# A two-layer trunk: where the second layer's S5 tables and first modulation vectors are made

## The chip, the cores and the metric

One core of a Trainium2 chip runs the whole kernel. The engines are TensorE (PE, with its weight loads as PEld), VectorE (DVE), ScalarE (ACT), GpSimd (POOL) and SyncE (SP), which here does nothing but issue transfers. The metric is the device time of one execution in microseconds (us), the median over the runs shown.

## The reference, cut to what matters

The input x is 512 tokens of 1024 channels, f32, and one conditioning vector c. Two layers follow one another, each of this form (names as in the reference, cut):

```
mod = silu(c) @ ada_w + ada_b                 # 6 vectors of 1024: shift, scale, gate, twice
h   = rms_norm(x, n1g) * (1 + scale1) + shift1
q, f, i, og, u, ga, gb = h @ w_in             # 56 blocks of 128 columns
a = hgrn2(q, f, i, og)                        # 8 heads, a gated linear recurrence in chunks of 32
s = gelu(s5(u)); s = s * sigmoid(s @ glu_w + glu_b)   # complex diagonal state space
x = x + gate1 * ((sigmoid(ga) * a + sigmoid(gb) * s) @ w_out)
h = rms_norm(x, n2g) * (1 + scale2) + shift2
x = x + gate2 * peer(h)                       # 16384 single-neuron experts, top 16 per head
```

The S5 branch of a layer depends on the layer's parameters alone (a, dt, B, C) for the small matrices with which it is applied: powers of the discretised diagonal, B times them, C times them. The kernel makes these matrices on the chip and calls them tables, 8 per layer, one for each unit of 128 channels. The modulation vectors depend on c and the layer's weights alone. Neither needs x.

## The kernel before, in words

**Precision and order.** Every f32 weight tile of 128x1024 is loaded by SP (tile `raw`), rounded by ACT into `whi` (L114), and DVE forms the rest, `wlo = raw - whi` (L116). Activations are split in the same way into `ahi` (L121, L229) and `alo` (L123, L231). Each product is three matmuls: hi by hi, lo by hi, hi by lo (L132 to L134, L145 to L147 in halves of the tokens, L1041 to L1043 for the V stage). A scheduler that works with a timeline of its own sets the order of instructions on every engine; the buffers of the tile pools decide when a tile may be written again, and a pool that opens in memory that another pool gave back waits for the last user of it. SP issues nearly all loads strictly in its order.

**One layer.** First the norm (L199 to L231), then the mixer: for each of 8 heads the projections, the HGRN2 head, an S5 unit with its table, ending in `yap` (L704); then the gates `ga` and `gb` (L732, L757), the gelu of S5, the glu products (L771 to L777) and the output products w_out with `merge` into x (L781 to L787). Of the eight w_out products five are whole and the last three are done in halves of 256 tokens, so that the second norm (`norm_mod_halves`, L235) can begin on the first half. Then PEER: wq and scores, top-16 selection, a dense matrix of gate values, the U stage (128 dense products with the U table, L795) and the V stage: a loop over 128 slices i, which loads a V tile, splits it, loads and gates the activations A (L1028 to L1032), and runs 24 matmuls of 128x384 into eight accumulators. The last 128 tokens are not done densely: POOL gathers rows of U and V by index (L957), and DVE multiplies and adds them (L967, L978). When all slices are done `into_x` (L1046) adds the accumulators to x.

**The tables.** `s5_small` (L277 to L397) makes, out of a and dt, some 190 small tiles of 128x32. `s5_maps` (L400 to L418) loads bre, bim, cre and cim and forms `bb` and `cc` of 128x512. `s5_build(sm, u, pv, pool, V, G)` (L432 to L482) fills one packed tile of 128x4352 for unit u: products of powers with bb and cc on DVE (L440 to L456), copies by ACT (L443, L464), and small products of 128 by 4 to 128x32 (L475 to L482) on the engine that is given as its last argument. `s5_tables` (L515 to L536) then transposes parts of the tile on PE and makes the matrices of the unit.

**Where this is done for layer 0 and for layer 1.** Layer 0's mixer calls `s5_maps` and `pack_tile` itself, and before each head builds the next head's table with DVE and POOL (`V, G`). Layer 1's tables are made ahead, during layer 0's V stage, by the generator `next_layer(1)` (L801 to L817): one step of it at each fourth slice. Its first step runs `s5_small`, opens the pool `bp`, runs `s5_maps` and `cond`, which makes csil = silu(c); a step then builds one table with DVE alone (`V, V`) and stores it to DRAM (`s5t`); after every second table four chunks of the modulation are made (`ada`, L161: load 128x1024, multiply by csil with a sum on DVE, L165), 16 chunks in all, which are the shift and the scale of the first norm. Layer 1's mixer loads one packed table per head (`pkl`, L713).

**The other chunks.** The 32 remaining chunks of a layer are made in its own mixer by `later(n)`: one in each ga step, three in each glu step, into the tag "ada" (two buffers) of the pool `gp`.

```
for i in range(n_end):                        # L1060, V stage
    w, g = spilled(i)
    for d in range(J):
        vmm(acc[d], d, w, g, i == 0, i == n1 - 1)
    gsteps(2 if i % 8 == 7 else 1)
    if i % 4 == 1:
        next(jobs, None)                      # a step of next_layer(1)
```

Of the kernel before, what the change touches and what calls it, by code (L numbers as in the profile page):

```python
# [4 lines left out]
F32 = mybir.dt.float32  # L5
# [12 lines left out]
J = 8  # L18
NB = 4
L = 2  # L20
# [21 lines left out]
def trunk(tc, a, dbg=None, layers=L, n_i2=128):  # L42
    nc = tc.nc
    V, S, G, TE = nc.vector, nc.scalar, nc.gpsimd, nc.tensor
    uid = [0]

    def nm(s):
        uid[0] += 1
        return f"{s}{uid[0]}"
# [350 lines left out]
    def s5_maps(l, sm, keep, pool, tags):  # L400
        E = V
        br, bi, tmp = (pool.tile([128, 32, 16], F32, tag=t, name=nm(t), bufs=1) for t in tags)
        nc.sync.dma_start(br, a["bre"][l])
        nc.sync.dma_start(bi, a["bim"][l])
        bb = [keep.tile([128, 32, 16], F32, name=nm("bb")) for _ in range(2)]
        zrb, zib = (z[:, :, None].to_broadcast([128, 32, 16]) for z in sm["z"])
        E.tensor_tensor(bb[0], zrb, br, op=OP.mult)
        E.tensor_tensor(tmp, zib, bi, op=OP.mult)
        E.tensor_tensor(bb[0], bb[0], tmp, op=OP.subtract)
        E.tensor_tensor(bb[1], zrb, bi, op=OP.mult)  # L410
        E.tensor_tensor(tmp, zib, br, op=OP.mult)
        E.tensor_tensor(bb[1], bb[1], tmp, op=OP.add)
        cc_ = [keep.tile([128, 32, 16], F32, name=nm("cc")) for _ in range(2)]
        nc.sync.dma_start(cc_[0], a["cre"][l])
        nc.sync.dma_start(cc_[1], a["cim"][l])
        S.activation(cc_[1], cc_[1], AF.Copy, scale=-1.0)
        sm.update(bb=bb, cc=cc_)

    su = drp.tile([L, J, 128, T], F32, name="su")
    sy = drp.tile([L, J, 128, T], F32, name="sy")  # L420
    s5t_ = {l: drp.tile([J, 128, 4352], F32, name=f"s5t{l}") for l in range(1, L)}

    PK = 4352

    def pack_tile(pool):
        t = pool.tile([128, PK], F32, name=nm("pk"))
        G.memset(t, 0.0)
        return t

    def pack_views(t):  # L430
        v = lambda o, m: t[:, o:o + 128 * m].rearrange("p (g m c) -> p g m c", g=4, c=32)
        w = lambda o: t[:, o:o + 512].rearrange("p (g n) -> p g n", g=4)  # L432
        return dict(wes=(v(0, 4), v(512, 4)), cas=(v(1024, 5), v(1664, 5)), bbr=(v(2304, 4), v(2816, 4)),
                    co=w(3328), si=w(3840))
# [49 lines left out]
    def mixer(l, h):  # L484
# [10 lines left out]
        sm = s5s[l]  # L495

        toe = fx.tile([128, 4, 4, 32], F32, name=nm("toe"))
        G.memset(toe, 0.0)
        if l == 0:
            s5_maps(l, sm, fx, hp, ("w1", "w2", "w3"))  # L500
            pk0 = pack_tile(fx)
        dcol = fx.tile([128, 32], F32, name=nm("dcol"))
        for j in range(4):
            nc.sync.dma_start(dcol[32 * j:32 * j + 32, :], a["dsk"][l])
# [200 lines left out]


        def tables(u):
            if l == 0:
                pv = pack_views(pk0)
                s5_build(sm, u, pv, hp, V, G)  # L710
            else:
                t = hp.tile([128, PK], F32, tag="pkl", name=nm("pkl"), bufs=1)
                nc.sync.dma_start(t, s5t_[l][u])  # L713
                pv = pack_views(t)
            return s5_tables(u, pv)

        tb_ = tables(0)
# [11 lines left out]
        def gates(n, pool, **kw):  # L729
            for _ in range(n):  # L730
                t = pool.tile([128, T], F32, name=nm("sgb"), **kw)
                S.activation(t, proj(48 + len(sgb)), AF.Sigmoid)  # L732
                sgb.append(t)

        if l == 0:
            gates(2, smp, tag="h", bufs=2)
        else:
            gates(J, yp)
        hctx.close()
        fx = mctx.enter_context(tc.tile_pool(name=f"gx{l}", bufs=1))  # L740
        hp = mctx.enter_context(tc.tile_pool(name=f"gp{l}", bufs=2))

        if l == 0:
            gates(J - 2, fx)
        else:
            cond(fx, stp)
        todo = list(range(16, 48))

        def later(n):
            n = min(n, len(todo))  # L750
            if n:
                ada(l, [todo.pop(0) for _ in range(n)], hp, "ada")

        for e in range(J):
            ps = proj(40 + e)
# [25 lines left out]
        def merge(e, ps, c=slice(0, T)):  # L781
            V.scalar_tensor_tensor(xT[:, e, c], ps[:, c], mod[l][:, 16 + e:17 + e], xT[:, e, c],
                                   op0=OP.mult, op1=OP.add)

        for e in range(J - 3):
            merge(e, dense(a["wout"][l, e], mg))
        dense_halves([a["wout"][l, e] for e in range(J - 3, J)], mg, lambda n, ps, c: merge(J - 3 + n, ps, c))  # L787
        mctx.close()
# [12 lines left out]
    def next_layer(l, fctx):  # L801
        with tc.tile_pool(name=f"s5s{l}", bufs=1) as t5:
            s5s[l] = s5_small(l, t5, lay[l])
        bp = fctx.enter_context(tc.tile_pool(name=f"bp{l}", bufs=1))
        s5_maps(l, s5s[l], bp, bp, ("cp1", "cp2", "md1"))
        pk = pack_tile(bp)
        cond(bp, stp)
        yield
        for u in range(J):
            s5_build(s5s[l], u, pack_views(pk), bp, V, V)  # L810
            nc.sync.dma_start(s5t_[l][u], pk)
            yield
            if u % 2:
                ada(l, list(range(2 * u - 2, 2 * u + 2)))
                yield
        gain1[l] = col(mod_gain(l, 1, vec["n1g"][:, l, :]))
        shift1[l] = col(mod[l])  # L817

# [401 lines left out]
```

## Time and profile before

| what | us |
|---|---|
| median of 3 runs (lowest to highest) | 3990.93 (3989.17 to 3995.62) |
| the profiled execution | 3988.25 |
| span in the trace | 3986.4 |
| layer 0: heads, yap of the first to yap of the last | 159 to 473 |
| layer 0: w_out, from the first merge to the first half of wq | 592 to 632 |
| layer 0: V stage, first gated slice to the first addition into x | 1421 to 2048 |
| layer 1: norm and first projections, up to yap of the first head | 2075 to 2164 |
| layer 1: heads | 2164 to 2476 |
| layer 1: V stage | 3429 to 3958 |

The profiled execution is 1.85 us longer than its span, and 2.68 us below the median. PE is busy for 94% of the span. In the two layers the same program runs with the same shapes, so a stage of layer 0 can be laid beside the same stage of layer 1; where the two differ in the work that is put beside the matmuls, the trace has both cases. The busy times below are those of an engine's instructions without counting overlaps twice, and the number in brackets is the count of instructions.

### The profile page before, as it was taken

How to read it: one execution, taken by the hardware profiler on the slowest of the kernel's cores; microseconds unless marked ns; L12 is line 12 of the kernel's file. 1: busy time of each engine (PE TensorE's matmuls, PEld its weight loads, DVE VectorE, ACT ScalarE, POOL GpSimd, SP SyncE). 2: the span in 40 equal slices, each digit the busy share in tenths (PEclk: the TensorE clock that was granted, in tenths of full speed). 3: DMA queues.
4: the chain of work that ended last, by engine and by line, in shares of the span. 5: the costliest groups of instructions: out<-in, count | busy, mean ns of one | idle time of the engine just before them, and what ended most of it. 6: DMA issues, size and time to landing. Idle time of an engine off the chain costs nothing.

```text
span 3986.4 us, 62595 instructions
## 1 busy us (share of the span) xinstructions
PE 3737.9 (94%) x21878; PEld 3500.6 (88%) x21878; DVE 3270.8 (82%) x9052; ACT 1577.6 (40%) x2510; POOL 883.7 (22%) x1139
## 2 busy tenths in 40 slices
PE   6999999999999766889999999999999998699998
PEld 5888878999999766888998888789999997699998
DVE  6998787999898889988757777869998988778874
ACT  3454543334343323334434444533334433233332
POOL 7454100022222433341000000000232223332210
PEclk9999999999999778999999999999999998799999
DMA  5222372488898899998743343723799998999984
GB/s 198 71 65 79 117 230 91 131 296 304 321 320 314 289 327 343 364 345 292 273 146 110 120 141 124 253 87 119 270 316 319 319 321 305 324 345 345 348 296 132
DMA packets 371212, 947.55 MB, mean 238 GB/s; under 512 B 36096, under 2 KB 187712, under 8 KB 368848
## 3 DMA queue, kind: packets, MB, share of 16 engines
q1 hardware_dynamic: 250144, 572.74, 42.5%
q0 software_dynamic: 73952, 268.56, 19.6%
q10 hardware_dynamic: 46800, 102.26, 6.7%
q8 instruction: 172, 2.82, 0.3%
q14 instruction: 144, 1.18, 0.1%
HBM read 814.44 MB, written 128.97 MB: 237 GB/s over the span
## 4 chain that ended last, share of the span: by engine, by line
PE 65%; DVE 16%; DMA 11%; issue 4%; ACT 2%; POOL 2%; ACTq 0%; SPq 0%; DVEq 0%; POOLq 0%
PE mm L133 11%; PE mm L132 11%; PE mm L134 11%; DVE wlo L116 3%; DMA gr<-v,idi 3%; PE mm L1042 2%; PE mm L1043 2%; PE mm L1041 2%; DMA gr<-ur,idi 2%; DVE jk L876 2%; DMA ada<-ada 2%; PE pa L1043 2%; PE pa L1042 2%; PE pb L1042 2%; PE pb L1043 2%
## 5 line engine op out<-in xcount | busy, mean ns | idle before, releaser
L114 ACT ACTIVATE whi<-raw 128x1024 fp32r<-128x1024 f32 x688 | 728.6, 1060 | 1354.1 <-PE mm L133 772.8
L133 PE MATMUL mm<-alo,whi 128*128 128x384 f32 (+1 forms) x3360 | 1213.7, 362 | 13.6 <-DVE alo L123 13.4
L134 PE MATMUL mm<-ahi,wlo 128*128 128x384 f32 (+1 forms) x3360 | 1214.1, 362 | 9.4 <-DVE wlo L116 9.1
L132 PE MATMUL mm<-ahi,whi 128*128 128x384 f32 (+1 forms) x3360 | 1213.0, 363 | 6.4 <-ACT ahi L229 5.6
L116 DVE TENSOR_TENSOR wlo<-raw,whi 128x1024 fp32r<-128x1024 f32 x688 | 840.2, 1222 | 254.5 <-ACT whi L114 239.1
L133 PEld LDWEIGHTS mm<-alo,whi 128*128 128x128 f32 x3360 | 636.0, 189 | 64.2 <-DVE alo L123 14.7
L134 PEld LDWEIGHTS mm<-ahi,wlo 128*128 128x128 f32 x3360 | 636.2, 189 | 61.1 <-DVE wlo L116 12.4
L132 PEld LDWEIGHTS mm<-ahi,whi 128*128 128x128 f32 x3360 | 636.6, 190 | 56.8 <-ACT ahi L229 7.1
L957 POOL DMA_INDIRECT gr<-ur,idi x256 | 278.1, 1086 | 1438.1 <-DVE jk L876 384.0
L957 POOL DMA_INDIRECT gr<-v,idi x256 | 362.2, 1415 | 662.7 <-DVE gacc L978 526.0
L978 DVE SCALAR_TENSOR_TENSOR gacc<-gr,gate,gacc 128x1024 f32<-128x1024 f32 x254 | 324.5, 1278 | 51.1 <-DMA gr<-v,idi 50.3
L1041 PE MATMUL mm<-gh,whi 128*128 128x384 f32 x768 | 227.3, 343 | 112.1 <-ACT whi L114 48.4
L967 DVE SCALAR_TENSOR_TENSOR gr<-gr,rows 128x1024 f32<-128x1024 f32 x256 | 311.0, 1217 | 17.6 <-DMA gr<-ur,idi 17.1
L1042 PE MATMUL mm<-gl,whi 128*128 128x384 f32 x768 | 260.9, 342 | 11.1 <-DVE gl L1032 11.0
L1043 PE MATMUL mm<-gh,wlo 128*128 128x384 f32 x768 | 255.9, 339 | 0.2 <-DVE wlo L116 0.2
L1041 PEld LDWEIGHTS mm<-gh,whi 128*128 128x128 f32 x768 | 142.5, 191 | 116.1 <-ACT gh L1030 66.0
L933 PE MATMUL pa<-Q,P 128*128 128x128 f16 x768 | 197.7, 296 | 43.7 <-DVE Q L927 41.1
L1030 ACT ACTIVATE gh<-A 128x384 fp32r<-128x384 f32 x256 | 132.1, 519 | 268.7 <-DVE A L1028 216.8
L876 DVE SCALAR_TENSOR_TENSOR jk<-iof,tf,ci 128x50 f32<-128x50 f32 x1024 | 223.9, 263 | 0.0
L935 ACT ACTIVATE stg<-pa 128x512 f32<-128x512 f32 x192 | 114.4, 598 | 223.3 <-PE pa L934 191.0
L934 PE MATMUL pa<-Q,P 128*128 128x128 f16 x768 | 187.9, 295 | 1.0
L1028 DVE TENSOR_TENSOR A<-A,W 128x384 f32<-128x384 f32 x256 | 139.2, 552 | 57.1 <-DMA A<-sA 52.0
(410 smaller groups left out, 6573.9 us busy)
## 6 DMA issues: line engine op xcount, KB each, us to landing
raw<-u SPq DMA_DIRECT2D x256, 512.0 KB
raw<-v SPq DMA_DIRECT2D x256, 512.0 KB
raw<-win SPq DMA_DIRECT2D x112, 512.0 KB
ada<-ada SPq DMA_DIRECT2D x96, 512.0 KB
sA<-uo ACTq DMA_DIRECT2D x256, 192.0 KB
sW<-stg ACTq DMA_DIRECT2D x64, 768.0 KB
A<-sA SPq DMA_DIRECT2D x256, 192.0 KB
W<-sW SPq DMA_DIRECT2D x64, 768.0 KB
```

Of the source, the lines that this page charges most:

```text
L114: S.activation(hi, raw, AF.Copy)
L116: V.tensor_tensor(lo, raw, hi[:].bitcast(F32), op=OP.subtract)
L132: TE.matmul(ps, hi[:, w], ah, start=(j == 0), stop=False)
L133: TE.matmul(ps, hi[:, w], al, start=False, stop=False)
L134: TE.matmul(ps, lo[:, w], ah, start=False, stop=(j == J - 1))
L876: V.scalar_tensor_tensor(jk, iof[:, 0:NCAND], tf[:, hh, k:k + 1], ci[:, hh], op0=OP.is_equal, op1=OP.mult, accum_out=code[:, hh, k:k + 1])
L957: G.indirect_dma_start(out=g[:], out_offset=None, in_=tab, in_offset=bass.IndirectOffsetOnAxis(ap=ids[:, s_:s_ + 1], axis=0))
L967: V.scalar_tensor_tensor(g, g, 1.0, rows, op0=OP.mult, op1=OP.mult, accum_out=dot[:, s_:s_ + 1])
L978: V.scalar_tensor_tensor(acc_, g, gate[:, s_:s_ + 1], acc_, op0=OP.mult, op1=OP.add)
L1041: TE.matmul(ps, w[0][:, c], g[0], start=first, stop=False)
L1042: TE.matmul(ps, w[0][:, c], g[1], start=False, stop=False)
L1043: TE.matmul(ps, w[1][:, c], g[0], start=False, stop=last)
```

## The change

The tables of layer 1 are no longer made in layer 0's V stage. Layer 1's mixer now does what layer 0's does: `s5_maps` and `pack_tile` at its start, and `s5_build` with `V, G` for each head. The DRAM tiles `s5t`, their stores and their loads are gone. `next_layer(1)` keeps `s5_small` and the two lines at its end. Six of the eight gb gates of layer 1 move from before to after the close of the heads' pools, as in layer 0. The 16 chunks of layer 1's first norm are made in layer 0's w_out loop: four before each of the first four whole products, in the two "ada" buffers, with layer 0's csil.

```
-        if l == 0:
-            s5_maps(l, sm, fx, hp, ("w1", "w2", "w3"))
-            pk0 = pack_tile(fx)
+        s5_maps(l, sm, fx, hp, ("w1", "w2", "w3"))
+        pk0 = pack_tile(fx)
...
         def tables(u):
-            if l == 0:
-                pv = pack_views(pk0)
-                s5_build(sm, u, pv, hp, V, G)
-            else:
-                t = hp.tile([128, PK], F32, tag="pkl", name=nm("pkl"), bufs=1)
-                nc.sync.dma_start(t, s5t_[l][u])
-                pv = pack_views(t)
+            pv = pack_views(pk0)
+            s5_build(sm, u, pv, hp, V, G)
             return s5_tables(u, pv)
...
-        def later(n):
+        follow = list(range(16)) if l + 1 < layers else []
+
+        def later(n, l_=l, todo=todo):
             n = min(n, len(todo))
             if n:
-                ada(l, [todo.pop(0) for _ in range(n)], hp, "ada")
+                ada(l_, [todo.pop(0) for _ in range(n)], hp, "ada")
...
         for e in range(J - 3):
+            later(4, l + 1, follow)
             merge(e, dense(a["wout"][l, e], mg))
...
     def next_layer(l, fctx):
         with tc.tile_pool(name=f"s5s{l}", bufs=1) as t5:
             s5s[l] = s5_small(l, t5, lay[l])
-        bp = fctx.enter_context(tc.tile_pool(name=f"bp{l}", bufs=1))
-        s5_maps(l, s5s[l], bp, bp, ("cp1", "cp2", "md1"))
-        pk = pack_tile(bp)
-        cond(bp, stp)
         yield
-        for u in range(J):
-            s5_build(s5s[l], u, pack_views(pk), bp, V, V)
-            nc.sync.dma_start(s5t_[l][u], pk)
-            yield
-            if u % 2:
-                ada(l, list(range(2 * u - 2, 2 * u + 2)))
-                yield
         gain1[l] = col(mod_gain(l, 1, vec["n1g"][:, l, :]))
```

**DVE in layer 0's V stage.** The names: gacc is the gathered sum of the last 128 tokens (L978 before, L957 after), A, gh and gl the gated activations (L1028 and L1032 before, L1007 and L1011 after), cp and md the table's products. Before:

```order
L165 SCALAR_TENSOR_TENSOR ada3870_17426,mod1_136<-ada3870_17426,csil3542_16003 128x1024
L1028 TENSOR_TENSOR A3889_17519<-A3889_17519,W3890_17521 128x384
L978 SCALAR_TENSOR_TENSOR gacc0_6543<-gr4296_19388,gate1864_8444,gacc0_6543 128x1024
L482 TENSOR_TENSOR pk3540_15999<-md3590_16227,md3591_16228 128x4x4
L456 TENSOR_TENSOR cp3641_16446<-pwr3494_15880,bb3536_15986 128x256
L165 SCALAR_TENSOR_TENSOR ada3871_17429,mod1_136<-ada3871_17429,csil3542_16003 128x1024
L1032 TENSOR_TENSOR gl3884_17484<-A3882_17479,gh3883_17482 128x384
L116 TENSOR_TENSOR wlo3874_17437<-raw3872_17433,whi3873_17435 128x1024
```

After, at the corresponding place:

```order
L1011 TENSOR_TENSOR gl3836_17597<-A3833_17590,gh3835_17595 128x384
L1007 TENSOR_TENSOR A3841_17632<-A3841_17632,W3834_17592 128x384
L116 TENSOR_TENSOR wlo3847_17670<-raw3845_17666,whi3846_17668 128x1024
L1011 TENSOR_TENSOR gl3843_17637<-A3841_17632,gh3842_17635 128x384
L957 SCALAR_TENSOR_TENSOR gacc0_6594<-gr4014_18604,gate1880_8495,gacc0_6594 128x1024
L116 TENSOR_TENSOR wlo3854_17710<-raw3852_17706,whi3853_17708 128x1024
```

Only the four operations of the stage itself are left there. The operations of `s5_small` still stand in the first slices.

**DVE in layer 0's w_out products.** xT is x, alo the low part of the merged activations, sg and ya the last glu gate and sum. Before:

```order
L123 TENSOR_TENSOR alo1240_5958<-ya0_675,ahi1239_5956 128x512
L116 TENSOR_TENSOR wlo1255_6036<-raw1253_6032,whi1254_6034 128x1024
L776 TENSOR_TENSOR sg1228_5932<-sg1228_5932,sgb1088_5174 128x512
L123 TENSOR_TENSOR alo1242_5962<-ya0_675,ahi1241_5960 128x512
L777 TENSOR_TENSOR ya0_675<-sg1228_5932,ya0_675 128x512
L123 TENSOR_TENSOR alo1244_5966<-ya0_675,ahi1243_5964 128x512
L782 SCALAR_TENSOR_TENSOR xT_112<-mm1248_5974,mod0_135,xT_112 128x512
L782 SCALAR_TENSOR_TENSOR xT_112<-mm1252_6006,mod0_135,xT_112 128x512
```

After (L765, L766 and L771 are the former L776, L777 and L782):

```order
L765 TENSOR_TENSOR sg1228_5931<-sg1228_5931,sgb1088_5173 128x512
L165 SCALAR_TENSOR_TENSOR ada1247_5973,mod1_135<-ada1247_5973,csil2_127 128x1024
L123 TENSOR_TENSOR alo1242_5961<-ya0_674,ahi1241_5959 128x512
L165 SCALAR_TENSOR_TENSOR ada1248_5976,mod1_135<-ada1248_5976,csil2_127 128x1024
L766 TENSOR_TENSOR ya0_674<-sg1228_5931,ya0_674 128x512
L167 TENSOR_TENSOR mod1_135<-mod1_135,v_adab_136 128x4
L165 SCALAR_TENSOR_TENSOR ada1253_6012,mod1_135<-ada1253_6012,csil2_127 128x1024
L123 TENSOR_TENSOR alo1244_5965<-ya0_674,ahi1243_5963 128x512
L165 SCALAR_TENSOR_TENSOR ada1254_6015,mod1_135<-ada1254_6015,csil2_127 128x1024
L165 SCALAR_TENSOR_TENSOR ada1255_6018,mod1_135<-ada1255_6018,csil2_127 128x1024
L771 SCALAR_TENSOR_TENSOR xT_112<-mm1252_5986,mod0_134,xT_112 128x512
```

The last two low parts that every w_out product needs, alo1242 and alo1244, now stand behind chunks of the next layer, each of which waits for its load. The sixteenth chunk stands among the merges of the halves.

**PE at the end of w_out.** L249 sums the squares of x for the second norm (pa the first half of the tokens, pb the second), L254 spreads its reciprocal root over the partitions, mm is the last w_out product. Before:

```order
L145 MATMUL mm1276_6148<-ahi1241_5960,whi1272_6142 128x256
L146 MATMUL mm1276_6148<-alo1242_5962,whi1272_6142 128x256
L254 MATMUL pa1308_6376<-ident_69,rsr1306_6365 128x128 x2
L147 MATMUL mm1276_6148<-ahi1241_5960,wlo1273_6144 128x256
L145 MATMUL mm1276_6148<-ahi1243_5964,whi1272_6142 128x256
L249 MATMUL pb1309_6379<-ones_79,sq1313_6392 128x1 x2
L249 MATMUL pb1309_6379<-ones_79,sq1314_6396 128x1 x2
L146 MATMUL mm1276_6148<-alo1244_5966,whi1272_6142 128x256
L147 MATMUL mm1276_6148<-ahi1243_5964,wlo1273_6144 128x256
```

After:

```order
L146 MATMUL mm1292_6199<-alo1244_5965,whi1288_6193 128x256
L147 MATMUL mm1292_6199<-ahi1243_5963,wlo1289_6195 128x256
L249 MATMUL pa1311_6379<-ones_79,sq1316_6396 128x1 x2
L249 MATMUL pa1311_6379<-ones_79,sq1317_6400 128x1 x2
L249 MATMUL pa1311_6379<-ones_79,sq1318_6404 128x1 x2
L249 MATMUL pa1311_6379<-ones_79,sq1319_6408 128x1 x2
L249 MATMUL pb1325_6430<-ones_79,sq1326_6431 128x1 x2
L249 MATMUL pb1325_6430<-ones_79,sq1327_6435 128x1 x2
L249 MATMUL pb1325_6430<-ones_79,sq1328_6439 128x1 x2
L249 MATMUL pb1325_6430<-ones_79,sq1329_6443 128x1 x2
L254 MATMUL pa1324_6427<-ident_69,rsr1322_6416 128x128 x2
```

The pool of the squares (`nq`) lies in memory of the "ada" buffers, so the first square waits for the sixteenth chunk. Half of the first half's sums and its L254 moved from inside the last w_out product to behind it.

## Rows read from the trace of the kernel before

**Rows 1.** The page, part 1: busy time, share of the span, instructions.

```profile
PE 3737.9 (94%) x21878; PEld 3500.6 (88%) x21878; DVE 3270.8 (82%) x9052; ACT 1577.6 (40%) x2510; POOL 883.7 (22%) x1139
```

**Rows 2.** Busy time by stretch, the two V stages (columns in the first row).

```profile
core 0: us, PE busy (x) PEld busy (x) DVE busy (x) ACT busy (x) POOL busy (x), PEclk, DMA share, GB/s
1421.00:1485.00 64.00, 62.55 (x335) 62.04 (x336) 58.51 (x163) 20.46 (x28) 24.79 (x17) 0.93 0.95 334
1485.00:1541.00 56.00, 16.32 (x83) 15.99 (x82) 50.91 (x129) 12.71 (x18) 23.81 (x20) 0.63 0.91 316
1541.00:1830.00 289.00, 256.10 (x1394) 250.33 (x1392) 261.55 (x522) 112.12 (x171) 100.28 (x71) 0.96 0.96 346
1830.00:2048.00 218.00, 217.27 (x1237) 215.83 (x1236) 149.25 (x326) 90.73 (x138) 5.66 (x11) 1.00 0.78 264
1421.00:2048.00 627.00, 552.23 (x3043) 544.18 (x3044) 520.22 (x1136) 236.03 (x352) 154.55 (x119) 0.94 0.89 313
3429.00:3958.00 529.00, 528.41 (x3043) 528.42 (x3044) 396.31 (x482) 193.73 (x253) 123.13 (x98) 1.00 0.88 312
```

**Rows 3.** Timeline of PE, then ACT, in layer 0's V stage (start, us).

```profile
1525.12 0.69 PE L1041 MATMUL mm<-gh,whi 128*128 128x384 f32 x1 [39.68 <-ACT whi L114]
...
1509.67 1.06 ACT L157 ACTIVATE csil<-ct 128x1024 f32<-128x1024 f32 x1 [20.22 <-DVE pp L395]
```

**Rows 4.** Groups of DVE, 1421 to 2048 (busy us, mean ns | idle before).

```profile
L165 DVE SCALAR_TENSOR_TENSOR ada<-ada,csil 128x1024 f32<-128x1024 f32 x16 | 19.3, 1217 | 0.0
L440 DVE TENSOR_TENSOR cp<-cp,cp 128x256 f32<-128x256 f32 (+1 forms) x32 | 14.4, 451 | 0.0
L475 DVE TENSOR_TENSOR md<-pk,pp 128x4 f32<-128x4 f32 (+6 forms) x56 | 12.8, 229 | 12.2 <-POOL pk L468 8.2 <-POOL pk L469 3.8
L286 DVE TENSOR_TENSOR s5s<-s5s,s5s 128x32 f32<-128x32 f32 x24 | 3.9, 181 | 0.0
```

**Rows 5.** Transfers, 1421 to 2048, then the sum of 3429 to 3958.

```profile
DMA packets 87281, 196.50 MB, mean 313 GB/s; under 512 B 6855, under 2 KB 54726, under 8 KB 86137
...
s5t<-pk SPq DMA_DIRECT2D x8, 2176.0 KB
ada<-ada SPq DMA_DIRECT2D x16, 512.0 KB
...
DMA packets 81801, 165.22 MB, mean 312 GB/s; under 512 B 6048, under 2 KB 53441, under 8 KB 81764
```

**Rows 6.** Busy time by stretch: heads of layer 0, heads of layer 1.

```profile
159.00:473.00 314.00, 310.32 (x1988) 270.65 (x1987) 274.19 (x593) 152.12 (x330) 123.98 (x288) 1.00 0.24 73
2164.00:2476.00 312.00, 312.00 (x2005) 273.93 (x2004) 232.10 (x523) 131.12 (x275) 3.46 (x20) 1.00 0.35 114
```

**Rows 7.** Groups, 39 to 473: the table's work in layer 0's mixer.

```profile
L476 POOL TENSOR_TENSOR md<-pk,pp 128x4 f32<-128x4 f32 (+6 forms) x56 | 33.4, 597 | 0.6
L443 ACT ACTIVATE pk<-cp 64x256 f32<-64x256 f32 (+1 forms) x64 | 28.2, 441 | 48.2 <-DVE cp L440 31.4 <-PE pb L586 16.4
L440 DVE TENSOR_TENSOR cp<-cp,cp 128x256 f32<-128x256 f32 (+1 forms) x32 | 17.3, 540 | 0.2
```

**Rows 8.** Timeline of PE at the layer boundary (start, us).

```profile
2059.52 1.04 PE L518 MATMUL pb<-ident,pkl 128*128 128x128 f32 x8
2062.72 3.76 PE L527 MATMUL pb<-pkl 128*128 128x128 f32 x16
2072.63 1.12 PE L199 MATMUL pc<-ident,rsr 128*128 128x128 f32 x4 [2.95 <-DVE rsr L192]
2075.34 1.22 PE L132 MATMUL mm<-ahi,whi 128*128 128x512 f32 x2 [1.59 <-ACT ahi L229]
```

**Rows 9.** Layer 0's w_out: busy time; then DVE and PE timelines.

```profile
592.00:632.00 40.00, 39.87 (x273) 36.69 (x271) 17.90 (x33) 13.48 (x25) 0.00 (x0) 1.00 0.30 93
...
546.68 1.23 DVE L165 SCALAR_TENSOR_TENSOR ada<-ada,csil 128x1024 f32<-128x1024 f32 x1 [2.06 <-DMA ada<-ada]
549.01 1.22 DVE L165 SCALAR_TENSOR_TENSOR ada<-ada,csil 128x1024 f32<-128x1024 f32 x1 [1.10 <-DMA ada<-ada]
...
622.78 0.16 DVE L177 TENSOR_SCALAR rsv<-pa 128x2 f32<-128x2 f32 x1
...
629.17 0.38 PE L254 MATMUL pa<-ident,rsr 128*128 128x128 f32 x2
...
631.43 0.48 PE L145 MATMUL mm<-ahi,whi 128*128 128x256 f32 x2
```

More of the change, by code (lines that the diff above doesn't have):

```diff
@@ L420, in trunk @@
     sy = drp.tile([L, J, 128, T], F32, name="sy")
-    s5t_ = {l: drp.tile([J, 128, 4352], F32, name=f"s5t{l}") for l in range(1, L)}
     PK = 4352
@@ L733, in gates @@
                 sgb.append(t)
[L735 to L738, printed above, removed]
+        gates(2, smp, tag="h", bufs=2)
         hctx.close()
@@ L741, in mixer @@
         hp = mctx.enter_context(tc.tile_pool(name=f"gp{l}", bufs=2))
-        if l == 0:
-            gates(J - 2, fx)
-        else:
+        gates(J - 2, fx)
+        if l > 0:
             cond(fx, stp)
         todo = list(range(16, 48))
-        def later(n):
+        follow = list(range(16)) if l + 1 < layers else []
+        def later(n, l_=l, todo=todo):
             n = min(n, len(todo))
             if n:
-                ada(l, [todo.pop(0) for _ in range(n)], hp, "ada")
+                ada(l_, [todo.pop(0) for _ in range(n)], hp, "ada")
         for e in range(J):
```

## The prediction

> **What bounds the kernel now.** I read the page's busy shares first: PE works for 94% of the span, DVE for 82% [rows 1]. So most of the kernel runs at PE's pace, and a change of DVE's work can only tell where PE stands still. To find such places I laid stage beside stage of the two layers in the view of busy time by stretch. The reader is to see that the V stage is the odd one: 627 us in layer 0, 529 us in layer 1, with the same count of matmuls (3043) in both [rows 2]. In layer 1 PE is busy for 528.41 of 529 us, so that stage is at PE's pace from end to end. In layer 0 PE is busy for 552.23 of 627. The 98 us of difference are what the extra work beside the matmuls costs in layer 0.
>
> Where they lie the stretches show. From 1485 to 1541 PE is busy for 16.32 of 56 us, and its clock falls to 0.63 of full speed [rows 2]; the timeline of PE has one stop of 39.68 us before 1525, released by ACT's whi [rows 3]. ACT stood still there because csil (L157), the first user of the pool bp, waited 20.22 us for DVE's last small tile of `s5_small` [rows 3], whose memory bp takes over; the following loads on SP and roundings on ACT queued behind it. From 1541 to 1830 PE is busy for 256.10 of 289 us while DVE is at 261.55 [rows 2]: there DVE, with the tables and chunks in its order among gl, A and wlo, is late again and again. After 1830 the jobs are over and PE is back at 217.27 of 218.
>
> **The change part by part.** The sum is made against the profiled execution, 3988.25 us; the median of the runs shown is 2.68 us above it, and I add that at the end.
>
> *Layer 0's V stage.* What goes from DVE: the tables and chunks, of which L440 (32 of 451 ns), L475 (56 of 229 ns, and five lines like it) and the 16 chunks (1217 ns each) are examples [rows 4]. All in all DVE is busy for 520.22 us in layer 0's stage and for 396.31 in layer 1's [rows 2], so 124 us are extra. What stays is `s5_small`: some 190 small operations of 181 ns, as L286 shows them [rows 4], that is some 34 us one after another, less where they overlap. csil, bp and with them the stop of 39.68 us go wholly. The transfers fall from 196.50 MB to about layer 1's 165.22 [rows 5]: 8 stores of 2176 KB and 16 chunks of 512 KB are 26 MB of the 31 that differ. Without the jobs the stage should come out as layer 1's: 627 - 529 = -98. `s5_small` costs something of it: in the first slices (1421 to 1485), where it ran among the gated slices in the old order too, PE was still busy for 62.55 of 64 us [rows 2], so 1.5 us; the new order spreads it thinner, over some 26 slices. Bounds: 0 and 34 (all of it on the path). I take +4. Term: -94.
>
> *Layer 1's heads, which now build their tables.* Layer 0's heads do exactly this: 314 us with PE busy for 310.32, against 312 and 312.00 in layer 1 [rows 6]. DVE rises from 232.10 to 274.19 and POOL from 3.46 to 123.98, and both stay beside PE. That cover is PE's projections; if it were gone each table would cost up to 15 us ((123.98 - 3.46)/8 of POOL). Bounds: 0 and +15, the latter if layer 1's tighter PE (no idle at all) lets each table's start show by 2 us. I take +4, the idle time of layer 0's PE. Here the Trainium skill speaks against the change. The trace shows L440 on DVE at 540 ns beside POOL's L476, which takes 597 ns [rows 7], and at 451 ns where both kinds were on DVE and L475 took 229 [rows 4]. SBUF — State Buffer, Who interferes with whom, says that a DVE instruction with two inputs from SBUF contends with a GpSimd instruction that reads SBUF, and that whoever comes second waits for the whole instruction; both tables' operations are of that kind, and the 20% agree. By the rule, if its wait reached PE, the heads would pay a fifth of DVE's extra 42 us (274.19 - 232.10), an estimate of +8, and the sum would be 3919; by the rows on the heads next to nothing of it reaches PE, and it stays at 3915.
>
> *The boundary between the layers.* Before, PE fills the gap between the last V matmul and the norm with the first table's transposes, 1.04 us of L518 and 3.76 us of L527, and then waits for DVE's rsr; the first projection starts at 2075.34 [rows 8]. After, bre, bim, cre and cim are loaded there, the maps and the first table's products stand among the small operations of the norm on DVE, and L527's work comes behind L199. Queued behind them are rsr, h and alo, and PE waits for these. Some ten DVE operations of 0.45 to 0.54 us [rows 4, 7] come between, 5 us, of which some fall into waits of the norm's own chain; and up to 3.76 us of PE move into a full stretch. Bounds 0 and +10; I take +5. The table itself is first wanted by PE near head 0's unit, some 80 us later.
>
> *Layer 0's w_out.* PE is full there (39.87 of 40 us), DVE is at 17.90 and the transfers at 93 GB/s [rows 9], so 16 x 1.217 = 19.5 us of DVE and 8 MB fit as such. But two things are moved. First, the low parts alo1242 and alo1244, which all w_out products need, stand behind five chunks, and with two buffers one chunk follows the other at 2.33 us (546.68 to 549.01, both waiting for their loads) [rows 9]. At worst PE waits for five of them, 12 us; it can meanwhile run three products up to that block, so I take +3. Second, the squares of the second norm wait for the sixteenth chunk. Half of the first half's sums and L254 now come behind the last w_out matmul. Before, rsv at 622.78 to L254 at 629.17 lay beside matmuls, and wq began at 631.43 [rows 9], 2.3 us after L254. After, PE has nothing between: the sums, the ten small operations (627 at the latest, so some 3 us without the operations between them), L254, h and ahi, 6 us together. Term: +9, bounds +3 and +18.
>
> *What costs nothing.* The loads of pkl (2176 KB per head) go; PE never waited in layer 1's heads [rows 6], so no gain. The gates are placed as in layer 0.
>
> Sum: -94 + 4 + 5 + 9 = -76; 3988.25 - 76 = 3912, and against the median 3990.93 - 76 = **3915 us**. With all terms at their good ends, -98 + 3 = -95: 3896. With all at their bad ends, -64 + 15 + 10 + 18 = -21: 3970; that they all come together is unlikely.
>
> **Rivals.**
>
> *The work is paid again where it goes* (each term's worse half at once): `s5_small` +19 in V, heads +10, boundary +8, w_out +15, against -98: -46, 3945 us. For it: PE has no slack in either place, and DVE was late beside far smaller loads. Against: layer 0's heads, which show the price at 2 us.
>
> *Only the stop goes.* If layer 0's V stage were slow for another reason than the jobs (what is left in it is gathered just as in layer 1, but its loads also run beside other traffic), the gain would be the stop before 1525 alone: -40 + 18 = -22, 3969 us. Against it: the stage is at PE's pace as soon as the jobs are over, with the same gather of the last tokens before 1830 in both layers.
>
> *Slower: the tables come late to each head of layer 1.* The mechanism is that unit e's table is begun only when the packed tile is free from unit e-1, so the POOL chain of 15 us per table stands on PE's path: 8 x 15 = +120 and 3990.93 - 76 + 120 = 4035 us. It decides from 9.5 us per table on (76/8). For it: there is one packed tile, where DRAM held eight. Against it: layer 0, with the same single tile, has PE idle for 3.7 us in all eight heads [rows 6].
>
> *The change doesn't do what it says*: jobs that are left in the V stage would keep the loss. The order on DVE shows none but `s5_small`, so I give this nothing of its own.
>
> **How the numbers follow.** My forecast 0.75 (its own range 3900 to 3930), the work paid again 0.13, only the stop 0.05, tables late 0.04, and 0.03 for things not thought of, half of them slower. 8 in 10 is held by 3894 to 3945. Faster by over 0.2% (8 us, what a measurement can tell from none) is 0.94, slower 0.05, between them 0.01.
>
> **What would show it.** The V stage of layer 0 at 530 to 540 us, with no stop over 5 us and PE's clock near 1.00; layer 1's heads at 312 to 318 with POOL near 124 busy; the first projection of layer 1 some 5 us later after the last V matmul than the 16 us of now; w_out of layer 0 with an idle PE of 3 to 6 us before wq. The prediction is wrong if the V stage stays over 560 us, if PE in layer 1's heads waits for L515, or if w_out grows by more than 18 us.

## The result and the profile after

| | us |
|---|---|
| changed kernel, median of 4 (lowest to highest) | 3932.16 (3930.45 to 3942.43) |
| kernel before, beside it | 3993.27 (3989.17 to 3998.01) |
| ratio, 95% interval | 0.9855 (0.9843 to 0.9868) |
| span in the trace, before and after | 3986.4, 3928.7 |

The kernel got 61 us faster by the medians and 57.7 by the traces; forecast were 76 (3915 us, range 3894 to 3945; the forecast's own range, 3900 to 3930, was missed by 2 us). The table lays the two traces beside each other. Each figure is the change of the time between two marks, so the column adds up: -57.2 of the span's -57.7. Both columns of times come from one trace each.

| stretch | before | after | change | forecast |
|---|---|---|---|---|
| layer 0, last ga to first scores (glu, w_out, start of wq) | 123.8 | 136.9 | +13.1 | +9 |
| layer 0, V stage: first gated slice to first addition into x | 626.4 | 537.7 | -88.7 | -94 |
| layer 1, from there to yap of the first head | 116.3 | 118.6 | +2.3 | +5 |
| layer 1, yap of the first to the last head | 312.1 | 317.9 | +5.8 | +4 |
| layer 1, last yap to last ga | 59.6 | 64.2 | +4.6 | 0 |
| layer 1, last ga to first gated slice (w_out, PEER) | 893.3 | 899.0 | +5.7 | 0 |

First the V stages, in the view of busy time by stretch (columns as in [rows 2]): the whole stage of layer 0, that of layer 1, then the first two stretches of layer 0.

```profile
1435.00:1973.00 538.00, 536.66 (x3044) 536.02 (x3045) 413.40 (x660) 193.23 (x253) 129.59 (x99) 0.99 0.89 313
3372.00:3901.00 529.00, 528.01 (x3042) 528.01 (x3042) 396.01 (x482) 192.53 (x253) 126.23 (x98) 1.00 0.88 311
1435.00:1503.00 68.00, 67.38 (x368) 67.38 (x369) 63.10 (x166) 23.61 (x32) 26.29 (x18) 0.95 0.98 348
1503.00:1573.00 70.00, 69.29 (x393) 68.65 (x392) 64.16 (x144) 24.39 (x32) 26.98 (x19) 1.00 0.97 350
```

The stop of [rows 3] is gone, and layer 0's PE is as full as layer 1's: 536.66 of 538 us. DVE has 17 us more than in layer 1 (`s5_small`), and PE lost 1.3 us in the two stretches where it runs. Still the stage is 9 us longer than layer 1's, with the same count of matmuls. A stage where PE is always busy can only be longer if the matmuls follow each other more slowly, and the count of them in equal stretches of 200 us shows it (layer 0, then layer 1, of the changed kernel):

```profile
1600.00:1800.00 200.00, 200.00 (x1141) 200.00 (x1140) 160.62 (x190) 74.20 (x95) 59.36 (x48) 1.00 0.94 343
3500.00:3700.00 200.00, 200.00 (x1155) 200.00 (x1155) 160.58 (x191) 73.62 (x95) 54.42 (x48) 1.00 0.96 346
```

1141 against 1155 is 175.3 against 173.2 ns from one matmul to the next, at a clock of 1.00 (the upper of its two levels, 2.4 GHz) in both: over the 3072 matmuls of a stage 6.5 us. This was there before the change too and has nothing to do with the jobs; what it is, two experiments below tell.

Then layer 0's w_out (stretches; the timelines of DVE, ACT and PE under them).

```profile
592.00:600.00 8.00, 6.15 (x28) 4.75 (x26) 3.91 (x6) 3.48 (x4) 0.00 (x0) 1.00 0.63 199
600.00:606.00 6.00, 3.54 (x8) 2.13 (x9) 5.73 (x9) 0.05 (x1) 0.00 (x0) 0.65 0.72 229
602.00:608.60 6.60, 5.35 (x12) 3.64 (x13) 6.60 (x10) 0.00 (x0) 0.00 (x0) 0.50 0.74 240
636.00:642.00 6.00, 5.21 (x35) 4.96 (x34) 3.41 (x14) 3.87 (x9) 0.00 (x0) 0.78 0.49 165
639.40:649.20 9.80, 9.74 (x46) 9.74 (x47) 7.70 (x25) 5.82 (x14) 0.00 (x0) 0.50 0.13 51
650.00:659.80 9.80, 9.80 (x84) 9.76 (x82) 5.17 (x16) 4.18 (x13) 0.00 (x0) 1.00 0.05 13
```

```profile
594.19 1.23 DVE L165 SCALAR_TENSOR_TENSOR ada<-ada,csil 128x1024 f32<-128x1024 f32 x1 [2.20 <-DMA ada<-ada]
...
595.34 0.69 DVE L123 TENSOR_TENSOR alo<-ya,ahi 128x512 fp32r<-128x512 f32 x1
...
599.16 1.23 DVE L165 SCALAR_TENSOR_TENSOR ada<-ada,csil 128x1024 f32<-128x1024 f32 x1 [0.94 <-DMA ada<-ada]
...
600.31 1.40 DVE L771 SCALAR_TENSOR_TENSOR xT<-mm,mod,xT 128x512 f32<-128x512 f32 x2
...
601.20 0.47 PE L132 MATMUL mm<-ahi,whi 128*128 128x512 f32 x1 [3.06 <-DVE xT L771]
...
628.78 0.73 ACT L247 ACTIVATE sq<-xT 128x256 f32<-128x256 f32 x2 [10.94 <-DVE ada L165]
...
641.18 0.67 PE L254 MATMUL pa<-ident,rsr 128*128 128x128 f32 x2
```

The last low part comes at 595.34, behind a chunk that waited 2.20 us for its load. PE goes on with what it has until 598.15, and its longest stop, 3.06 us, ends not with a low part but with the first merge (L771): DVE does it at 600.31, behind two more chunks that waited for their loads; before, it ran at 592. In all PE stands still for 4.3 us between 592 and 606. The squares begin at 628.78, released by the last chunk, and L254 comes at 641.18, after the last product. What the forecast had no term for is in the column of the clock. After the first stop PE has the lower of its two levels, 0.50 (1.2 GHz), from 602 to 608.6. It has it again from 639.4 to 649.2, after some 4 us in which it ran only the one-column sums (L249) and stood still for 0.8; there it is busy nearly all the time and runs 46 matmuls, and 84 in the same time at 1.00 right after. Before, the clock was 1.00 throughout [rows 9].

Layer 1's mixer: heads and the stretch behind them, then PE's waits, and one of ACT's, where the last head ends.

```profile
2091.30:2409.20 317.90, 312.72 (x2006) 273.31 (x2004) 268.48 (x589) 158.16 (x337) 124.14 (x284) 1.00 0.24 72
2409.20:2473.40 64.20, 62.23 (x266) 51.08 (x266) 46.36 (x76) 41.23 (x49) 0.00 (x0) 0.96 0.85 280
```

```profile
2407.38 1.03 PE L199 MATMUL pc<-ident,rsr 128*128 128x128 f32 x4 [3.33 <-DVE rsr L192]
...
2410.09 1.58 ACT L724 ACTIVATE sgb<-mm 128x512 f32<-128x512 f32 x3 [5.96 <-DVE ya L701]
...
2410.74 0.80 PE L132 MATMUL mm<-ahi,whi 128*128 128x512 f32 x1 [2.34 <-ACT sgb L724]
```

The heads look like layer 0's [rows 6], with 5 us of PE idle, 3.33 of which are the first of the two waits at the end (the stretch ends at 2409.2). Both waits are new: the last head's norm, and a gate's product that finds no free accumulator. The tiles of the gates from the third on now lie in the pool `gx`, in memory that the heads give back, so ACT waits 5.96 us for the last yap (ya) before it takes three gates' products out of their accumulators. In the old order PE had the products of all eight gb gates to put there.

### The profile page after: what moved, and what is told of

It reads as the page before. It is cut to its first block, busy times and chain, and to the rows that moved or that the text cites. A ratio compares the mean times of both kernels' runs of the same rounds, so it can differ in the third digit from the quotient of the medians.

```text
span 3928.7 us, 62542 instructions
## 1 busy us (share of the span) xinstructions
PE 3736.3 (95%) x21878; PEld 3502.1 (89%) x21878; DVE 3238.6 (82%) x8715; ACT 1574.6 (40%) x2507; POOL 1021.7 (26%) x1475
## 4 chain that ended last, share of the span: by engine, by line
PE 77%; DVE 11%; DMA 7%; POOL 2%; issue 2%; ACT 1%; SPq 0%; ACTq 0%; DVEq 0%; POOLq 0%
PE mm L132 12%; PE mm L133 12%; PE mm L134 12%; PE mm L1021 3%; PE mm L1020 3%; PE mm L1022 3%; PE pb L1021 2%; PE pa L1022 2%; PE pb L1020 2%; PE pa L1021 2%; PE pa L1020 2%; PE pb L1022 2%; DMA ada<-ada 2%; DVE wlo L116 2%; PE pa L912 2%; PE pa L913 2%
## 5 line engine op out<-in xcount | busy, mean ns | idle before, releaser
L134 PE MATMUL mm<-ahi,wlo 128*128 128x384 f32 (+1 forms) x3360 | 1216.7, 363 | 10.5 <-DVE wlo L116 10.4
L936 POOL DMA_INDIRECT gr<-ur,idi x256 | 269.5, 1053 | 1481.4 <-DVE jk L855 764.6
L936 POOL DMA_INDIRECT gr<-v,idi x256 | 350.6, 1370 | 669.1 <-DVE gacc L957 583.0
L957 DVE SCALAR_TENSOR_TENSOR gacc<-gr,gate,gacc 128x1024 f32<-128x1024 f32 x254 | 324.5, 1277 | 45.3 <-DMA gr<-v,idi 45.0
L1020 PE MATMUL mm<-gh,whi 128*128 128x384 f32 x768 | 210.0, 338 | 50.6 <-ACT gh L1009 26.4
L1020 PE MATMUL pb<-gh,whi 128*128 128x384 f32 x512 | 172.8, 338 | 0.0
```

What stands on the lines that cost most here:

```text
L134: TE.matmul(ps, lo[:, w], ah, start=False, stop=(j == J - 1))
L936: G.indirect_dma_start(out=g[:], out_offset=None, in_=tab, in_offset=bass.IndirectOffsetOnAxis(ap=ids[:, s_:s_ + 1], axis=0))
L957: V.scalar_tensor_tensor(acc_, g, gate[:, s_:s_ + 1], acc_, op0=OP.mult, op1=OP.add)
L1020: TE.matmul(ps, w[0][:, c], g[0], start=first, stop=False)
```

## Experiments

The theory is the sum above: the V stage gains what the jobs cost (a stop, and DVE late), and the three places where the work now is pay for it. The rivals were that one part of the jobs did all the harm, that the prices of the new places are not what I named, and, for the V stage's 9 us, place in memory against chance. All ratios are to the kernel before on the same chip.

### Tables alone, chunks alone, and the stop alone

Tables alone, the 16 chunks stay in the V stage:

```
         s5s[l] = s5_small(l, t5, lay[l])
+        bp = fctx.enter_context(tc.tile_pool(name=f"bp{l}", bufs=1))
+        cond(bp, stp)
         yield
+        for u in range(J):
+            yield
+            if u % 2:
+                ada(l, list(range(2 * u - 2, 2 * u + 2)))
+                yield
...
-            later(4, l + 1, follow)
```

> The tables move to the second mixer, the 16 chunks stay as jobs in layer 0's V stage (csil made there as before). Theory (the jobs cost DVE time and a stop, each its own amount): w_out of layer 0 is back at the old kernel's times (13 us less than in the changed kernel), the 16 chunks of 1.2 us hide beside PE, and the V stage has the stop for csil alone, 20 to 40 us over the changed kernel's 538; in all some 3950 us. Rival (the chunks were what made DVE late): V stage over 590 us and in all 3975 or more. Rival (no price for the chunks in either place): 3932.

Measured: 3958.13 us, ratio 0.9918 (0.9893 to 0.9943). The V stage takes 581.7 us, w_out is back at the old times (39 us from first to last merge), the mixer pays as in the changed kernel. In the stretch around the stop and on PE (columns as before):

```profile
1485.00:1541.00 56.00, 22.36 (x115) 22.36 (x116) 48.37 (x107) 11.91 (x14) 26.09 (x20) 0.66 0.89 318
```

```profile
1518.64 0.69 PE L1026 MATMUL mm<-gh,whi 128*128 128x384 f32 x1 [37.37 <-ACT whi L114]
...
1506.28 1.06 ACT L157 ACTIVATE csil<-ct 128x1024 f32<-128x1024 f32 x1 [19.60 <-DVE pp L395]
```

The stop is there without any table: 37.37 us, behind csil, which waits 19.60 us for the memory of `s5_small`'s tiles. The 44 us that this V stage has over the changed kernel's are nearly all this one stop (forecast were 20 to 40); the chunks themselves hide.

Chunks alone (the kernel before, without csil and chunks in `next_layer`, and with the four lines of the change in w_out):

> The chunks move to w_out, the tables are made and stored in layer 0's V stage as before. Theory: w_out pays its 13 us here too, the second mixer pays nothing, and the V stage keeps nearly all that the tables cost on DVE: 590 to 610 us against 627, in all some 3975 to 3985. Rival (the loads and stores decide, 26 MB of which the stores are 18): V stage falls by the chunks' 8.4 MB, 24 us, and w_out's 13 us are all that is lost: 3980, with PE idle spread evenly. Rival (the stop is all): without csil on ACT no stop, V stage near 585, in all 3960.

Measured: 3965.2 us, ratio 0.9932 (0.9909 to 0.9956). w_out pays 13 us here too. The V stage takes 585.2 us:

```profile
1500.00:1556.00 56.00, 54.37 (x306) 53.42 (x305) 54.25 (x136) 20.79 (x29) 24.92 (x17) 1.00 0.98 356
1556.00:1845.00 289.00, 259.49 (x1392) 252.75 (x1392) 257.75 (x512) 112.67 (x175) 121.11 (x75) 0.96 0.95 339
```

No stop from 1500 to 1556, and then, with the tables alone, the same loss as in [rows 2]: 259.49 of 289 us. So csil's stop together with the chunks is worth 41 to 44 us and the tables' work 45 to 47.5, and -45 and -41 from the two experiments add up to -86, nearly the -89 of the change. The theory's 590 to 610 us for the stage, and 3975 to 3985 in all, were too long. The rival that the stop is all is near in the stage's length, but the rows show that the time is lost elsewhere; the rival that the loads and stores decide fails, with 41 us less in the stage and not 24.

The stop alone, in the kernel before: `bp` is opened beside the small tiles, not in their memory.

```
-        with tc.tile_pool(name=f"s5s{l}", bufs=1) as t5:
-            s5s[l] = s5_small(l, t5, lay[l])
         bp = fctx.enter_context(tc.tile_pool(name=f"bp{l}", bufs=1))
+        t5 = fctx.enter_context(tc.tile_pool(name=f"s5s{l}", bufs=1))
+        s5s[l] = s5_small(l, t5, lay[l])
```

> The kernel before, with the pool of the table work placed beside the memory of the small tiles and not in it, so that csil need not wait. Theory (stop and late DVE are separate losses): the stop of 39.68 us before slice 16 goes, V stage 590, in all 3955. Rival (DVE is the bound of the first 400 us, and was busy for 50.91 of 56 us in the stop as well): the work only moves, V stage 610 to 625, in all 3980 to 3990.

Measured: 3975.24 us, ratio 0.9959 (0.9946 to 0.9973); the V stage 615.7 instead of 626.4. The trace is of the slowest of nine runs (3982.65), so by the medians the gain is 16 us.

```profile
1487.00:1543.00 56.00, 47.68 (x238) 46.29 (x239) 50.83 (x134) 20.32 (x31) 27.07 (x11) 0.91 0.84 289
1423.00:2039.00 616.00, 559.87 (x3041) 547.38 (x3042) 518.98 (x1134) 231.72 (x350) 175.60 (x118) 0.97 0.90 319
```

PE's stop is gone (47.68 of 56, before 16.32), and the stage gains only 11 us. The rival holds for the stage (610 to 625), though the median lies 5 us below its 3980: while all jobs are there DVE has 519 us of work and had used the stop for it, 50.91 of its 56 us [rows 2]. A stop during which the scarce engine works is not time to be had; it becomes so only when that engine's work goes too, as in the chunks' experiment.

### What w_out pays for

The chunks loaded into the four `raw` buffers:

```
-            later(4, l + 1, follow)
+            if follow:
+                ada(l + 1, [follow.pop(0) for _ in range(4)])
```

> The changed kernel, with the 16 chunks loaded into the four raw buffers of the weights and not into the two buffers whose memory the second norm's squares take over. Theory (w_out's 13 us come from the squares that wait for the sixteenth chunk, and from low parts queued behind chunks that wait for one of two buffers): the squares and L254 lie inside the products again, w_out pays 2 to 6 us instead of 13, in all 3921 to 3926. Rival (19.5 us more of DVE in 40 us, or the 8 MB of loads, are the price themselves): still 11 to 15 us, 3932; it could be more, since the weights then wait for the chunks' buffers.

Measured: 3930.95 us, ratio 0.9843 (0.9819 to 0.9868), no different from the changed kernel. The squares lie inside the products again, and scores come 11.4 us late instead of 13.1. ACT, PE and DVE around the last low part:

```profile
595.21 1.06 ACT L114 ACTIVATE whi<-raw 128x1024 fp32r<-128x1024 f32 x1 [10.12 <-DMA raw<-wout]
...
596.32 0.50 PE L132 MATMUL mm<-ahi,whi 128*128 128x512 f32 x1 [2.22 <-ACT whi L114]
...
599.56 0.69 DVE L123 TENSOR_TENSOR alo<-ya,ahi 128x512 fp32r<-128x512 f32 x1
```

The low parts now stand behind even more chunks, and the last of them is done at 600.25. But that is not what PE waits for most: from 575 to 612 it waits 4.2 us for whi, 1.1 for low parts and 0.6 for wlo. The weights of w_out come late, since their loads stand among the chunks' on SP and share the four buffers with them, and the first merge comes 13 us late. The theory falls, and the rival named both its 11 to 15 us and this wait: freeing the squares only exchanges the old waits for another. What DVE's order alone would cost, with the loads out of the way, stays open.

The chunks late in the V stage instead:

```
         s5s[l] = s5_small(l, t5, lay[l])
+        for _ in range(24):
+            yield
+        bp = fctx.enter_context(tc.tile_pool(name=f"bp{l}", bufs=1))
+        cond(bp, stp)
         yield
+        for q in range(4):
+            ada(l, list(range(4 * q, 4 * q + 4)))
+            yield
...
-            later(4, l + 1, follow)
```

> The changed kernel, with the 16 chunks taken out of w_out and made late in layer 0's V stage, four after each of the slices 101, 105, 109 and 113, when the gathers are over and DVE is busy for 55% and the transfers for 68%; csil is made after slice 97. Theory (chunks are free where DVE, SP and the loads have room, and w_out's 13 us are the chunks'): w_out is back at the old times, -13 us, the V stage grows by 0 to 4, in all 3918 to 3924. Rival (csil stops ACT and SP wherever it is made in the V stage): a stop of PE of 10 us or more after slice 97, in all 3930 or more.

Measured: 3922.69 us, ratio 0.9825 (0.9804 to 0.9845). w_out, and the end of the V stage; then PE early in that stage:

```profile
592.00:632.00 40.00, 40.00 (x273) 36.96 (x271) 16.87 (x30) 11.97 (x20) 0.00 (x0) 1.00 0.27 87
1850.00:1961.00 111.00, 110.93 (x631) 110.61 (x630) 77.88 (x119) 40.38 (x54) 0.00 (x0) 1.00 0.85 290
```

```profile
1544.16 0.44 PE L1026 MATMUL mm<-gh,whi 128*128 128x384 f32 x1 [1.43 <-ACT gh L1015]
...
1558.91 0.44 PE L1026 MATMUL mm<-gh,whi 128*128 128x384 f32 x1 [1.43 <-ACT gh L1015]
```

w_out is full and at full clock. The chunks lie beside matmuls that wait for nothing (110.93 of 111); csil finds its memory free and stops nobody. The stage as a whole is 542 us, 4 more than in the changed kernel, but 2.9 of these are two stops of PE, 1.43 us each, some 280 us before csil is made and the first chunk runs. Both kernels with late chunks below have the same two stops; why the new order of the stage brings them is not shown.

### What the second mixer pays for

Two of the six late gates moved ahead:

```
-        gates(2, smp, tag="h", bufs=2)
+        if l == 0:
+            gates(2, smp, tag="h", bufs=2)
+        else:
+            gates(2, yp)
+            gates(2, smp, tag="h", bufs=2)
...
-        gates(J - 2, fx)
+        gates(J - len(sgb), fx)
```

> The changed kernel, with two more of the second mixer's gb gates made before the close of the heads' pools (two in the pool of yap, two in the buffers h, four behind, instead of two and six). Theory (the 4.6 us between the last yap and the last ga of the second mixer come from PE, which has no product of gates left to fill the last head's waits for rsr and for a buffer h): PE's waits of 3.3 and 2.3 us go, 3 to 5 us less, in all 3928. Rival (the table work on DVE is what delays the last head): no change in that stretch.

Measured: 3921.23 us, ratio 0.9820 (0.9795 to 0.9846); first to last head and to the last ga:

```profile
2092.00:2414.90 322.90, 321.82 (x2049) 281.13 (x2048) 271.15 (x590) 162.31 (x343) 124.08 (x284) 1.00 0.24 74
2414.90:2466.30 51.40, 50.76 (x224) 41.67 (x223) 36.78 (x60) 39.91 (x45) 0.00 (x0) 1.00 0.80 277
```

PE idles 1.7 us over both stretches instead of 7.2, and the clock of the second is 1.00 instead of 0.96. The sum of the two is 374.3 instead of 382.1 us, where the kernel before had 371.7; 3 to 5 us had been expected of the edit. So most of the heads' 5 us of idle PE, too, was a lack of products to put into the last head's waits; some 1 us of it is left.

The tables by DVE alone:

```
-            s5_build(sm, u, pv, hp, V, G)
+            s5_build(sm, u, pv, hp, V, G if l == 0 else V)
```

> The changed kernel, with the second mixer's tables built by DVE alone instead of DVE and POOL. DVE takes over six groups of 56 operations of about 230 ns, 77 us in eight heads, where it is busy for 268 of 318 us now. Theory (PE's 5.7 us over the old heads come from DVE and the chain of the table): DVE comes close to PE and the heads grow by 10 to 40 us, in all 3942 to 3972. Rival (by the rule on the shared port DVE and POOL hinder each other so much that POOL's help is worth nothing): the products of 256 and 320 columns return from 540 to 450 ns, and the heads stay or get shorter, 3925 to 3935.

Measured: 3927.0 us, ratio 0.9838 (0.9816 to 0.9859). The heads by busy time, then one group of DVE's products in them (busy us, mean ns; here, then in the changed kernel):

```profile
2090.20:2409.90 319.70, 315.27 (x2006) 276.12 (x2004) 292.22 (x840) 159.83 (x337) 4.73 (x32) 0.99 0.23 71
```

```profile
L438 DVE TENSOR_TENSOR cp<-cp,cp 128x320 f32<-128x320 f32 (+1 forms) x21 | 9.5, 453 | 0.0
```

```profile
L438 DVE TENSOR_TENSOR cp<-cp,cp 128x320 f32<-128x320 f32 (+1 forms) x21 | 10.1, 480 | 0.2
```

The rival is nearer: with 24 us more of DVE work the heads are 1.8 us longer. POOL's help is worth next to nothing here. Beside POOL this group's mean is 480 instead of 453 ns, 6% more, and that costs as little.

### Why matmuls are 175.3 ns apart in one layer and 173.2 in the other

```
+        if l + 1 == layers:
+            pad = vctx.enter_context(tc.tile_pool(name="padv", bufs=1))
+            pd = pad.tile([128, 1120], F32, name="padt")
+            G.memset(pd[:, 0:1], 0.0)
         vp = vctx.enter_context(tc.tile_pool(name=f"vp{l}", bufs=2))
```

> The changed kernel, with an unused tile of 4480 bytes per partition ahead of the second layer's V stage pool, so that its activations gh and gl, its A and W lie at the same places as in layer 0's V stage (where the pool of the S5 small tiles takes these 4480 bytes). It tests why matmuls that follow one another without a stop are 175.6 ns apart in layer 0's V stage and 173.3 ns in layer 1's. Theory (the place in memory decides): layer 1's become 175 to 176 ns, its V stage 7 us longer. Rival (what else runs, or the data): 173.3 as before.

In the second kernel the tile is filled with zeros and used once:

```
+            G.memset(pd, 0.0)
+            V.tensor_tensor(xT[:, 0, :], xT[:, 0, :], pd[:, 0:T], op=OP.add)
```

> The changed kernel, with a tile of 4480 bytes per partition of zeros ahead of the second layer's V stage pool, which is added once to one block of x, so that it is surely kept; A, W, gh and gl of layer 1 lie exactly where layer 0 has them. Theory (the place decides the distance of the matmuls): 175.6 to 176.0 ns in layer 1 as well, its V stage 7 to 8 us longer, in all 3940. Rival (the longer distance of the run with the unused tile was of that execution alone): 173.3 ns, 3932.

Measured: 3939.46 and 3940.5 us, one time each; layer 1's V stage is 8.0 and 7.2 us longer than in the changed kernel. Layer 1, 200 us, in the second of the two kernels:

```profile
3500.00:3700.00 200.00, 200.00 (x1141) 200.00 (x1140) 159.97 (x190) 72.72 (x94) 53.89 (x47) 1.00 0.94 341
```

1141, as in layer 0. So, together with the last kernel below, which makes layer 0 faster by such a tile, the place of the stage's tiles in memory sets the distance of the matmuls.

### The two helpful edits together, and layer 0's tiles moved

The edits for the late chunks and for the gates, as shown above, in one kernel:

> The changed kernel with both edits that helped alone: the 16 chunks late in layer 0's V stage, and four gb gates of the second mixer before the close of its heads' pools. Theory (the two places are independent): w_out back at the old times, the second mixer 7 us shorter than in the changed kernel, the V stage 0 to 4 longer; 3932 - 13 + 4 - 7 = 3916, ratio to the kernel before 0.980 to 0.982. Rival (the first of the two only moved its cost, as its run alone came out at 3922.7 and not lower): 3921 to 3925.

And with a tile ahead of layer 0's pool:

```
+        if l + 1 < layers:
+            pad = vctx.enter_context(tc.tile_pool(name="padv", bufs=1))
+            pd = pad.tile([128, 928], F32, name="padt")
+            G.memset(pd[:, 0:1], 0.0)
```

> As the run before it, with an unused tile of 3712 bytes per partition ahead of layer 0's V stage pool, so that A, W, gh and gl of layer 0 lie 8192 bytes beyond their places in layer 1, and no longer 4480. Theory (the place decides the distance of the matmuls, and it goes by the place modulo some power of two up to 8192): 173.3 ns in layer 0 too, V stage 7 us shorter, in all 3909. Rival (place decides, but otherwise): 175 to 176 ns as now, 3916. Rival (place decides nothing): the same 3916.

Measured: 3911.86 us, ratio 0.9802 (0.9789 to 0.9816), and 3906.93 us, ratio 0.9791 (0.9778 to 0.9804). Layer 0's V stage, 200 us, in the second:

```profile
1600.00:1800.00 200.00, 200.00 (x1155) 200.00 (x1155) 162.54 (x194) 74.47 (x97) 57.74 (x48) 1.00 0.96 344
```

1155 in layer 0 as well; its V stage is 536.3 us, in the kernel without the tile 541.9. The two edits add up as the theory has it. The times of these last two kernels are too near to each other to be told apart by their intervals; the traces' V stages are not. Both beat the kernel before and the changed kernel.

## Why the prediction came out as it did

The direction, the place of the gain and the range were right; the gain was forecast at 76 and was 61, because terms of the sum were mis-sized, nearly all the same way. The total, 3932, even lies nearer to the rival of work paid again (3945) than to 3915. By the parts that rival is not borne out: only w_out came near its price, and it had no price for the gates and PEER, which moved the total besides.

- **V stage, -94 forecast, -88.7.** I took layer 1's stage as what layer 0's would become. The stop and the lateness went as said. But some 7 us of the difference of the two stages are the slower sequence of matmuls, which no job causes and which stayed. Of my +4 for `s5_small` about 1.3 us are seen as idle PE. [rows 2] had the hint: layer 0 at full clock and without jobs made 1237 matmuls in 217.27 busy us (1830 to 2048), layer 1 3043 in 528.41, that is 175.6 and 173.6 ns.
- **w_out, +9 forecast, +13.1.** L254 came behind the last product, as said. The low parts stood behind chunks, as said, but PE had other products and waited only 0.5 us for one, at 582; the 3.06 and 0.98 us of its stops behind them were for merges, which DVE did only after more chunks. Forecast were 3 us, measured 4.3: the size is nearly right by luck, for another wait. What I missed besides is the clock. An estimate from the rows: 46 matmuls in 9.8 us against 84 at 1.00 are 4.4 us, and 12 in the first slow stretch, 0.43 us apart instead of 0.23, are 2.4; with 5.1 us of idle PE that makes 12 of the 13.1.
- **Boundary, +5 forecast, +2.3.** The maps slowed h and alo (from first to last ahi 15.1 instead of 9.2 us), but the first projection was not late, and PE made up for half.
- **Heads, +4 forecast, +5.8**, and **the gates, 0 forecast, +4.6.** "The gates are placed as in layer 0" was true and no reason for a price of nothing: in layer 1's old order they had filled the last head's waits. This is the step whose mechanism failed; the gates' experiment gave 7.8 of these 10.4 us back.
- **Layer 1's w_out and PEER, 0 forecast, +5.7.** Not explained. 3.3 us of it lie between the last gelu of the U stage and the first gated slice, a stretch whose change came out between -0.6 and +4.4 us in the other kernels' single traces; no experiment ties it to the change. In the eleven traces of kernels without an edit in it, the two of the table among them, the stretch takes from 890.2 to 899.0 us, so the difference of two single traces may be chance.
- **The shared port** could have cost up to +8. In the changed kernel's second mixer L438 takes 480 ns against 453 without POOL, and taking POOL away gained nothing in the heads. Over all 32 products of L438 in layer 1 the shortest are alike, 403 and 404 ns, but the longest are 830 and 495: a few are held up for long. The trace agrees with the rule of the Trainium skill (SBUF — State Buffer, Who interferes with whom) that the two engines hinder each other. It does not show the price on PE.

## What to carry to other kernels

A stage of one layer laid beside the same stage of another is a good price list, but count the matmuls in a stretch where PE never stops in both, before the difference is put down to the extra work. Moved work should go to where the engine, the queue and the memory are all free, and not in front of something that a full engine waits for: 16 chunks cost 13 us in w_out and under 0.3 us of idle PE late in the V stage. And work that "moves to where the other layer has it" also leaves a place, where it may have been filling waits.

## What the runs showed of the hardware that I had not expected

- The matmuls 128x384 of the V stage follow one another in 175.3 or 173.2 ns (1141 or 1155 in 200 us), both at a granted clock of 1.00 (2.4 GHz), depending on where A, W, gh and gl lie: with these 4480 bytes further on per partition the slower, at the old place or 8192 bytes beyond it the faster. It was moved in both directions. Which tile of them it is, and by what rule, stays open.
- After a stop of PE of 3.06 us the granted clock was 0.50 from 602 to 608.6, and after some 4 us of one-column sums with 0.8 us of idle time it was 0.50 from 639.4 to 649.2, where PE was busy for 9.74 of 9.80 us. The matmuls 128x512 came 0.43 us apart in the first of these stretches and 0.23 before the stop. So a wait costs more than itself.
